# The expert stage of a two-block model on one core: a fixed TensorE order, biases in batches, and a last unit that joins as products

## The chip, the cores and the metric

The kernel runs on one core of a Trainium2 chip. A core has five engines with queues of their own: TensorE (PE), VectorE (DVE), ScalarE (ACT), GpSimd (POOL) and SyncE (SP, which here only issues transfers), and sixteen DMA engines. An engine takes the instructions of its queue in order. The metric is the device time of one launch in microseconds (us); less is better.

## What is computed

Two transformer blocks over T = 512 tokens of width D = 1024, all in float32. The first block has a mixer (a gated delta rule and sliding-window attention) and then 32 experts, of which each token takes four; the second has attention, an MLP, a recurrent layer and an MLP. The change lies in the experts:

```python
def _moe(h, w_router, b_router, w_up, b_up, w_down, b_down):
    logits = xf @ w_router + b_router              # 512 tokens, 32 experts
    top_val, top_idx = lax.top_k(logits, 4)
    gates = softmax(top_val)
    ...
    def expert_block(xb, e):                       # rows of one expert
        hu = xb @ w_up[e] + b_up[e]                # 1024 -> 2048
        x_glu = minimum(hu[:, :1024], 7.0)
        x_lin = clip(hu[:, 1024:], -7.0, 7.0)
        act = x_glu * sigmoid(1.702 * x_glu) * (x_lin + 1.0)
        return act @ w_down[e] + b_down[e]         # 1024 -> 1024
    ys = ys * row_gate[:, None]
    return segment_sum(ys, row_tok, num_segments=T)

x = x + gate2 * _moe(h, ...)
```

The weights of the experts are 384 MB (up 8 MB, down 4 MB for each expert), and all of them are read.

## The kernel before

**Ranks and units.** The experts are ranked by their count of tokens. A table, UNITS (L36), lays the ranks out in blocks of 128 rows: a block holds one expert (`_single`) or two (`_pair(a, b, n)`: n rows for a, the rest for b). One or two blocks that are worked on together are a step, one or two steps a unit; there are ten units with 20 blocks. Two of the units are a single step of two blocks (ranks 2 and 14, ranks 3 and 6). A rank's row count that the table doesn't hold goes to a loop over further blocks behind the second unit (LOOP, L1465), which runs zero times for these inputs. The last unit has the steps 23/24 and 13/31.

**One step.** `gather_T` (L1132) makes the transposed rows of a unit, xT, with products of the token matrix and 0/1 columns ("hot"). `expert_up` (L1159) makes for each quarter j of the 2048 columns a product in a PSUM bank "hu": first a product that puts in the biases (L1166), then the products with the weights (`tiled`, L1129), in tiles of 32, 64 or 128 columns by how the block is divided. DVE and ACT then apply the activation (L1176 to L1180: five operations, one on ACT), in place and into "ma". `transposed` (L1183) turns ma in eight transposes (L1188) and two copies (L1189) into aT, `expert_down` (L1192) makes the down product in two PSUM banks (hu for the second block of a step), and `expert_out` (L1203) scales the rows by their gates (ACT, L1208) and has POOL scatter them to y_d in DRAM (L1211). y_d has four slots for each token, 2048 rows in all. `slots` (L1113) makes row numbers and gates for the next unit. The down product of a step stands behind the up product of the step after it, in the code.

**What sets the order.** The code is written engine by engine in this sequence, but a scheduler orders each engine's queue, by dependencies and its own estimate, so PE's instructions of neighbouring steps are mixed. The weight loads (1 MB each, 384 of them) go to SP's queue in the order of the code, into thirteen buffers "raw" (L305). The hu banks are four, shared by all j and by the second block's down product.

**Ends of the stage.** Ahead of the stage SP fills half of y_d with zeros (L867, rows of slots that may stay empty). At its start the routing makes Z (positions and gates), transposes it (L1319), permutes it by rank (L1323) and derives R, selE and the like. `expert_bias` (L1397), called behind the first step of the last unit, adds the down biases to xs, the rows of the residual stream in h2h. At the end (L1472 on): SP loads the four slots of all tokens from y_d (`load_y`, L1474: 16 loads of 512 KB, four into h2l and twelve into raw buffers), DVE sums them (L1479), PE makes the last down product, that of 13/31, whose rows join as products with the hot columns instead of by a scatter (`add_rows`, L1215; products L1500 and L1501), and DVE adds these, multiplies by g2bc (gate2) and adds to xs (L1502 to L1504). The next stage starts with transposes of xs (L1580) and its weight loads on SP (L305).

## Time and profile before

| | us |
|---|---|
| median of the three runs | 2954.44 (2952.50 to 2954.49) |
| the profiled execution | 2947.46 |
| its span | 2945.2 |
| expert stage, first gather to first transposes of the next stage | 466.1 to 1613.4 |
| up to the end of the down product of 23/24 | 1549.4 |
| no PE work | 1549.4 to 1579.4 |
| last down product | 1579.4 to 1600.4 |
| sums to the next stage | 1600.4 to 1613.4 |

The profile shows one execution. Times in the timeline are counted from the start of its span. A timeline row gives the start, the length, the engine, the line, the operation with what it writes and reads, how many were run together, and in brackets the idle time before it and what ended that. A float32 product of the tiles here shows as two records in the trace: a quarter j of an up product of a block in tiles of 32 is 32 instructions and x64 in the timeline. A group's length runs to the modelled end of its last product; the next can start a little earlier, so distances between starts are the better measure.

### The profile page before, as it was taken

What the parts mean: (1) busy time and instruction counts of PE and PEld (TensorE: products, weight loads), DVE (VectorE), ACT (ScalarE), POOL (GpSimd) and SP (SyncE); (2) the same over time, 40 slices, a digit from 0 to 9 for tenths busy, and PEclk for the clock granted to TensorE, in tenths of its full rate; (3) what the DMA queues carried; (4) which work ended last, traced back from release to release, by engine and by line L of the source; (5) the groups of instructions that cost most, each with busy time, mean ns of one, the idle gap of its engine ahead of it and who ended that gap; (6) DMA issues with size and microseconds to landing.
All of it is one profiled execution on the core that took longest, in us unless ns stands there. A gap on an engine that the chain in (4) does not pass through costs nothing. (4 is left out here: it accounts for less than half of the span.)

```text
span 2945.2 us, 36638 instructions
## 1 busy us (share of the span) xinstructions
PE 2696.4 (92%) x14288; PEld 1713.3 (58%) x14288; DVE 1459.0 (50%) x2445; ACT 787.0 (27%) x1333; POOL 576.7 (20%) x401
## 2 busy tenths in 40 slices
PE   6889998998999999999994988999999899699997
PEld 4667875443434333333331756877877677588886
DVE  5996475211211111111124567676568788954446
ACT  4343341000000000000001553323235555332221
POOL 2340041000000000000000314233232333622223
PEclk8989998999999999999997998999998999799999
DMA  7544037797999997999986631565323222132331
GB/s 283 184 167 153 29 132 300 276 421 294 370 396 419 390 392 304 406 374 405 417 338 250 202 115 65 200 222 179 109 83 102 72 83 82 64 122 84 100 104 50
DMA packets 126209, 643.46 MB, mean 218 GB/s; under 512 B 16217, under 2 KB 17197, under 8 KB 76880
## 3 DMA queue, kind: packets, MB, share of 16 engines
q1 hardware_dynamic: 122064, 632.32, 57.0%
q0 software_dynamic: 3824, 8.25, 0.7%
q8 instruction: 113, 1.85, 0.3%
q14 instruction: 64, 0.52, 0.1%
q10 hardware_dynamic: 144, 0.52, 0.0%
HBM read 624.47 MB, written 18.45 MB: 218 GB/s over the span
## 5 line engine op out<-in xcount | busy, mean ns | idle before, releaser
L1129 PE MATMUL bank_hu<-raw,xT 128*32 128x512 f32 (+2 forms) x3456 | 618.2, 601 | 0.0
L1129 PEld LDWEIGHTS bank_hu<-raw,xT 128*32 128x32 f32 (+2 forms) x3456 | 190.0, 123 | 345.5 <-issue 336.4
L1603 POOL TENSOR_TENSOR h2h<-h2h,yt 128x512 f32<-128x512 f32 x161 | 239.5, 1494 | 679.7 <-DVE yt L1602 669.8
L319 DVE TENSOR_TENSOR wl<-raw,wh 128x1024 fp32r<-128x1024 f32 (+1 forms) x209 | 299.9, 1444 | 111.5 <-ACT wh L314 110.7
L314 ACT CAST wh<-raw 128x1024 fp32r<-128x1024 f32 (+1 forms) x231 | 236.8, 1042 | 399.1 <-PE bank_u L324 178.3
L1129 PE MATMUL bank_y<-raw,aT 128*32 128x512 f32 (+2 forms) x1536 | 294.7, 599 | 31.6 <-DMA raw<-in_w_down_dram 31.6
L1176 DVE TENSOR_SCALAR ma<-bank_hu 128x256 f32<-128x256 f32 x80 | 34.0, 425 | 561.3 <-PE bank_hu L1129 561.3
L324 PE MATMUL bank_u<-h_lo,wh 128*128 128x512 f32 (+1 forms) x680 | 250.8, 370 | 9.0 <-DVE h_lo L1587 9.0
L323 PE MATMUL bank_u<-h_hi,wh 128*128 128x512 f32 (+1 forms) x680 | 251.6, 372 | 7.1 <-ACT wh L314 4.1
L325 PE MATMUL bank_u<-h_hi,wl 128*128 128x512 f32 (+1 forms) x680 | 251.2, 370 | 3.6 <-DVE wl L319 3.6
L1211 POOL DMA_INDIRECT y_d<-yb,ii x19 | 18.6, 977 | 998.9 <-ACT yb L1208 865.8
L1129 PEld LDWEIGHTS bank_y<-raw,aT 128*32 128x32 f32 (+2 forms) x1536 | 95.5, 123 | 199.2 <-issue 189.4
L323 PE MATMUL bank_d<-wh,a 128*128 128x512 f32 x512 | 203.0, 397 | 3.5 <-DVE yt L1602 3.5
L1602 DVE TENSOR_TENSOR yt<-bank_d,G 128x512 f32<-128x512 f32 x168 | 113.4, 687 | 183.9 <-PE bank_d L325 178.3
L324 PE MATMUL bank_d<-wl,a 128*128 128x512 f32 x512 | 201.7, 394 | 0.7 <-DVE wl L319 0.7
L325 PE MATMUL bank_d<-wh,b 128*128 128x512 f32 x512 | 198.4, 394 | 1.0 <-DVE b L1822 1.0
L1177 ACT ACTIVATE mb<-ma 128x256 f32<-128x256 f32 x80 | 33.3, 417 | 582.2 <-DVE ma L1176 582.2
L324 PEld LDWEIGHTS bank_u<-h_lo,wh 128*128 128x128 f32 x680 | 130.4, 192 | 31.8 <-DVE h_lo L1587 9.8
L323 PEld LDWEIGHTS bank_u<-h_hi,wh 128*128 128x128 f32 x680 | 130.4, 193 | 29.2 <-ACT wh L314 4.5
L325 PEld LDWEIGHTS bank_u<-h_hi,wl 128*128 128x128 f32 x680 | 130.4, 192 | 26.1 <-DVE wl L319 3.8
L323 PEld LDWEIGHTS bank_d<-wh,a 128*128 128x128 f32 x512 | 96.7, 189 | 28.3 <-DVE yt L1602 5.2
L393 DVE SCALAR_TENSOR_TENSOR gacc<-graw,sc,gacc 128x1024 f32<-128x1024 f32 x67 | 91.4, 1364 | 42.5 <-DMA graw<-in_ada_w_dram 33.6
(568 smaller groups left out, 4403.3 us busy)
## 6 DMA issues: line engine op xcount, KB each, us to landing
raw<-in_w_up_dram SPq DMA_DIRECT2D x256, 1024.0 KB, 10.3
raw<-in_w_down_dram SPq DMA_DIRECT2D x128, 1024.0 KB, 12.6
raw<-in_mlp_w_dram SPq DMA_DIRECT2D x128, 512.0 KB, 4.4
graw<-in_ada_w_dram SPq DMA_DIRECT2D x72, 512.0 KB, 3.7
graw<-in_w_ada_dram SPq DMA_DIRECT2D x48, 512.0 KB, 4.5
raw<-in_ada_w_dram SPq DMA_DIRECT2D x24, 512.0 KB, 3.8
raw<-in_rnn_w_in_dram SPq DMA_DIRECT2D x24, 512.0 KB, 3.7
raw<-in_w_in_dram SPq DMA_DIRECT2D x22, 512.0 KB, 4.5
```

What stands on the lines that cost most here:

```text
L314: act.copy(out=h, in_=r)
L319: vec.tensor_tensor(out=l, in0=r, in1=h.bitcast(F), op=OP.subtract)
L323: pe.matmul(out=o, lhsT=lhs[0], rhs=rhs[0], start=first, stop=False)
L324: pe.matmul(out=o, lhsT=lhs[0], rhs=rhs[1], start=False, stop=False)
L325: pe.matmul(out=o, lhsT=lhs[1], rhs=rhs[0], start=False, stop=last)
L393: vec.scalar_tensor_tensor(out=acc, in0=r, scalar=w, in1=acc, op0=OP.mult, op1=OP.add)
L1129: pe.matmul(out=o[at + a:at + a + tile], lhsT=lhs[:, a:a + tile], rhs=rhs, start=start, stop=stop, tile_position=(0, at + a))
L1176: vec.tensor_scalar(out=a, in0=hu[:, 0:256], scalar1=7.0, scalar2=None, op0=OP.min)
L1177: act.activation(out=b, in_=a, func=AF.Tanh, scale=0.851)
L1211: pool.indirect_dma_start(out=y_d, out_offset=bass.IndirectOffsetOnAxis(ap=sl[0][:, 0:1], axis=0), in_=yb, in_offset=None, bounds_check=4 ...
L1602: vec.tensor_tensor(out=t, in0=ps, in1=G[:, cs], op=OP.mult)
L1603: eng.tensor_tensor(out=xs[tb][:, cs], in0=xs[tb][:, cs], in1=t, op=OP.add)
```

## The change

Eight things change, all in the expert stage.

1. The table of units is in a new order; the two units of two blocks now stand fifth and ninth (third and seventh before). The label permutation (which kept ranks 13 and 31 last) is gone, and ranks are used directly.
2. `pin` ties each PE instruction of the stage to the one pinned before it, in the order of the code. Pinned are biases, gathers, slots, weight products, transposes and the new late products; the routing transposes and expert_bias aren't.
3. The biases of a step are batched: all four j of a one-block step at its start, in the order 0, 2, 1, 3; for a two-block step j = 0 and 1 at the start, and j = 2 and 3 ahead of its third quarter.
4. The slots of the next unit are made between j = 1 and j = 2 of the last step.
5. The zero fill covers all of y_d, 16 loads rather than 8.
6. `add_slots`, called behind the first step of the last unit, loads the sixteen slot rows on POOL's queue into three pairs of buffers (two pairs in h2l, one in xT), and for each pair adds the two, multiplies by g2bc, and adds to xs: 24 DVE operations of 1024 columns.
7. Both blocks of the last unit, 23/24 and 13/31, join xs as products (`late_rows`, `late_add`), by halves of the width: DVE scales and multiplies by g2bc, ACT casts, DVE subtracts for the low part, PE makes two products into an hu bank for each of four token blocks, DVE adds to xs.
8. `load_y`, `sum_y` and the old tail are gone.

```diff
 UNITS = [
     [_single(0), _single(1)],
     [_pair(7, 25, 96), _pair(8, 26, 96)],
+    [_pair(15, 16, 64), _single(4)],
+    [_pair(9, 27, 96), _pair(17, 18, 64)],
     [[[(2, 0, 128, 0)], [(2, 0, 64, 128), (14, 64, 64, 0)]]],
-    [_pair(15, 16, 64), _pair(9, 27, 96)],
...
     [_pair(23, 24, 64), _pair(13, 31, 96)],
 ]
-LABELS = [r for r in range(32) if r not in (13, 31)] + [13, 31]
...
-    for tb in range(8, 16):
+    for tb in range(16):
         sync.dma_start(out=y_d[tb * 128:tb * 128 + 128, :]...
...
+    def pin(x):
+        if pinned[0] is not None:
+            tc.add_manual_dep(x.ins, pinned[0].name, mybir.DependencyInfo(
+                mybir.DependencyClass.NoSync, mybir.DependencyReason.DATA), reason="order")
+        pinned[0] = x.ins
...
+    def expert_up(srcs, biases, blocks, get=fetch, between=None):
         acts_ = [mt([128, 1024], "ma", 3, F, mo) for _ in blocks]
+        banks = {}
         for j in range(4):
-            hus = [pbank("hu") for _ in blocks]
-            q = slice(j // 2 * 64, j // 2 * 64 + 64)
-            for hu, bs in zip(hus, biases):
-                pe.matmul(out=hu, lhsT=bs[q], rhs=bup[q, j % 2 * 512:j % 2 * 512 + 512], start=True, stop=False)
+            if j not in banks:
+                js = (0, 2, 1, 3) if len(blocks) == 1 else (j, j + 1)
+                banks.update((j_, [pbank("hu") for _ in blocks]) for j_ in sorted(js))
+                for j_ in js:
+                    q = slice(j_ // 2 * 64, j_ // 2 * 64 + 64)
+                    for hu, bs in zip(banks[j_], biases):
+                        pin(pe.matmul(out=hu, lhsT=bs[q], rhs=bup[q, j_ % 2 * 512:j_ % 2 * 512 + 512], start=True,
+                                      stop=False))
+            if j == 2 and between is not None:
+                between()
+            hus = banks[j]
...
+    def late_rows(b):
+        hotT = mt([128, 1024], "ma", 3, FR, mo)[:, 0:512]
         pt = trbank()
         for tb in range(NTB):
+            pin(pe.matmul(out=pt[:, tbs[tb]], lhsT=hots[-1][:, tb, 128 * b:128 * b + 128].bitcast(F), rhs=ident,
+                          start=True, stop=True))
         act.copy(out=hotT, in_=pt)
+        return hotT
+
+    def late_add(y, gc, hotT):
+        yh, yl = (mt([128, 8, 128], "aT", 3, FR, mo).rearrange("p a b -> p (a b)") for _ in range(2))
         t_ = mt([128, 1024], "yb", 2, F, mo)
         for h in range(2):
             hs = slice(h * 512, h * 512 + 512)
+            vec.scalar_tensor_tensor(out=t_[:, hs], in0=y[h], scalar=gc, in1=g2bc[:, hs], op0=OP.mult, op1=OP.mult)
+            act.copy(out=yh[:, hs], in_=t_[:, hs])
+            vec.tensor_tensor(out=yl[:, hs], in0=t_[:, hs], in1=yh.bitcast(F)[:, hs], op=OP.subtract)
+            for tb in range(NTB):
+                o = pbank("hu")
+                pin(pe.matmul(out=o, lhsT=hotT[:, tbs[tb]], rhs=yh[:, hs], start=True, stop=False))
+                pin(pe.matmul(out=o, lhsT=hotT[:, tbs[tb]], rhs=yl[:, hs], start=False, stop=True))
+                vec.tensor_tensor(out=xs[tb][:, hs], in0=o, in1=xs[tb][:, hs], op=OP.add)
...
+    def add_slots():
+        spare = mt([128, 8, 256], "xT", 2).rearrange("p a b -> p (a b)")
+        pairs_ = [[h2_("l", 0), h2_("l", 1)], [h2_("l", 2), h2_("l", 3)], [spare[:, 0:1024], spare[:, 1024:2048]]]
+        for tb in range(NTB):
+            for j in (0, 2):
+                y = pairs_[0]
+                pairs_.append(pairs_.pop(0))
+                for i, t in enumerate(y):
+                    pool.dma_start(out=t, in_=y_d[(j + i) * T + tb * 128:(j + i) * T + tb * 128 + 128, :])
+                vec.tensor_tensor(out=y[0], in0=y[0], in1=y[1], op=OP.add)
+                vec.tensor_tensor(out=y[0], in0=y[0], in1=g2bc, op=OP.mult)
+                vec.tensor_tensor(out=xs[tb], in0=xs[tb], in1=y[0], op=OP.add)
...
+            late = not nxt and n
+            if late:
+                hotT = late_rows(n - 1)
             if prev is not None:
                 for y, sl in zip(expert_down(*prev[:2]), prev[2]):
                     finish()
-                    finish = expert_out(y, sl)
+                    if late:
+                        late_add(y, sl[1], hotT)
+                    else:
+                        finish = expert_out(y, sl)
...
             if not nxt and n == 0:
                 expert_bias()
+                add_slots()
...
-    load_y(ys[0], 0)
...
+    hotT = late_rows(1)
+    late_add(expert_down(*prev[:2])[0], prev[2][0][1], hotT)
```

How the instructions stand on the engines, in three places. In the rows, a name's number is that of its buffer.

PE before, one step in the middle of the stage (transposes of the step ahead, biases, up products bank_hu, slots bank_tr from R, then the down product bank_y):

```order
L1188 MATMUL bank_tr<-ident,ma 128x128 x8
L1166 MATMUL bank_hu<-bup,bs 128x512
L1129 MATMUL bank_hu<-raw,xT 32x512 x15
L1129 MATMUL bank_tr<-R,hot 128x2 x4
L1129 MATMUL bank_hu<-raw,xT 32x512 x17
L1166 MATMUL bank_hu<-bup,bs 128x512
L1129 MATMUL bank_hu<-raw,xT 32x512 x32
L1166 MATMUL bank_hu<-bup,bs 128x512
L1129 MATMUL bank_hu<-raw,xT 32x512 x32
L1166 MATMUL bank_hu<-bup,bs 128x512
L1129 MATMUL bank_hu<-raw,xT 32x512 x32
L1129 MATMUL bank_y<-raw,aT 128x512 x16
```

PE after, two steps of the same unit and its slots:

```order
L1203 MATMUL bank_tr<-ident,ma 128x128 x8
L1177 MATMUL bank_hu<-bup,bs 128x512 x4
L1134 MATMUL bank_hu<-raw,xT 32x512 x128
L1134 MATMUL bank_y<-raw,aT 128x512 x16
L1203 MATMUL bank_tr<-ident,ma 128x128 x8
L1177 MATMUL bank_hu<-bup,bs 128x512 x4
L1134 MATMUL bank_hu<-raw,xT 32x512 x64
L1134 MATMUL bank_tr<-R,hot 64x2 x8
L1134 MATMUL bank_tr<-R,hot 128x2 x4
L1134 MATMUL bank_hu<-raw,xT 32x512 x64
```

The four biases moved to the front of the step, and the up product is cut only by the slots of the next unit, at its half.

SP before, behind the first eight of the last sixteen down loads:

```order
L305 DMA raw<-in_w_down_dram 128x2048
L1474 DMA h2l_9937<-y_d 128x1024
L1474 DMA h2l_9938<-y_d 128x1024
L1474 DMA h2l_9939<-y_d 128x1024
L1474 DMA h2l_9940<-y_d 128x1024
L1474 DMA raw<-y_d 128x1024 x12
L305 ISA
L305 DMA raw<-in_w_down_dram 128x2048
```

After, the sixteen loads from y_d are gone from SP (the down loads follow each other) and stand on POOL behind its last scatter.

DVE after, behind the activations of the last up product (13/31): L1246 and L1248 scale and split the rows of 23/24, L1457 to L1459 are the sums of the slots, L1253 the additions of the late products:

```order
L1248 TENSOR_TENSOR aT<-yb,aT 128x512
L1246 SCALAR_TENSOR_TENSOR yb<-bank_y,gc,g2bc 128x512
L1248 TENSOR_TENSOR aT<-yb,aT 128x512
L1457 TENSOR_TENSOR h2l_9661<-h2l_9661,h2l_9662 128x1024
L1458 TENSOR_TENSOR h2l_9661<-h2l_9661,g2bc 128x1024
L1459 TENSOR_TENSOR h2h_9603<-h2h_9603,h2l_9661 128x1024
L1457 TENSOR_TENSOR h2l_9663<-h2l_9663,h2l_9664 128x1024
L1458 TENSOR_TENSOR h2l_9663<-h2l_9663,g2bc 128x1024
L1457 TENSOR_TENSOR xT<-xT 128x1024
L1459 TENSOR_TENSOR h2h_9603<-h2h_9603,h2l_9663 128x1024
L1458 TENSOR_TENSOR xT<-xT,g2bc 128x1024
L1253 TENSOR_TENSOR h2h_9603<-bank_hu,h2h_9603 128x512
```

All 24 sums stand behind the scaling of 23/24, and the eight late additions of 23/24 stand among them, the last two behind the last sum. On PE the sixteen late products of 23/24 (L1251, L1252) stand behind its down product and ahead of the transposes and the down product of 13/31.

## Rows read from the trace of the kernel before

**Rows 1.** The page, its first line.

```profile
span 2945.2 us, 36638 instructions
```

**Rows 2.** Windows: stretch, length; PE, PEld, DVE, ACT, POOL; clock, DMA, GB/s.

```profile
1200.00:1533.10 333.10, 322.17 (x2010) 116.91 (x2009) 60.08 (x133) 26.39 (x50) 9.56 (x9) 0.99 0.99 403
...
1549.40:1579.40 30.00, 0.03 (x1) 0.02 (x1) 14.71 (x12) 0.69 (x1) 0.97 (x1) 0.54 0.86 339
1579.40:1600.40 21.00, 19.32 (x128) 5.60 (x128) 0.00 (x1) 0.80 (x2) 0.00 (x0) 0.93 0.79 329
1600.40:1613.40 13.00, 4.02 (x17) 2.94 (x17) 11.91 (x16) 1.72 (x3) 0.00 (x0) 0.86 0.00 0
```

**Rows 3.** Timeline of PE, third and fourth blocks: start, length, line, operation, count.

```profile
563.89 3.63 PE L1129 MATMUL bank_hu<-raw,xT 128*32 128x512 f32 x30
567.45 1.05 PE L1129 MATMUL bank_tr<-R,hot 128*128 128x2 f32 x8
568.43 4.48 PE L1129 MATMUL bank_hu<-raw,xT 128*32 128x512 f32 x34
572.85 0.50 PE L1166 MATMUL bank_hu<-bup,bs 64*128 64x512 f32 x1
573.27 7.07 PE L1129 MATMUL bank_hu<-raw,xT 128*32 128x512 f32 x64
580.28 0.50 PE L1166 MATMUL bank_hu<-bup,bs 64*128 64x512 f32 x1
...
595.14 14.00 PE L1129 MATMUL bank_y<-raw,aT 128*128 128x512 f32 x32
608.98 1.04 PE L1188 MATMUL bank_tr<-ident,ma 128*128 128x128 f32 x8
```

**Rows 4.** Waits from 466 to 1613: us in total, times, the longest.

```profile
PE bank_tr L1188 <- DVE ma L1180: 14.8, 11, 2.0
```

**Rows 5.** Timeline, an activation chain on DVE, and products of PE behind such a wait.

```profile
1502.13 0.42 DVE L1176 TENSOR_SCALAR ma<-bank_hu 128x256 f32<-128x256 f32 x1 [1.67 <-PE bank_hu L1129]
...
1503.56 0.43 DVE L1180 SCALAR_TENSOR_TENSOR ma<-bank_hu,ma 128x256 f32<-128x256 f32 x1
...
1513.77 5.32 PE L1129 MATMUL bank_hu<-raw,xT 128*32 128x512 f32 x26
```

**Rows 6.** Timeline of PE, start of the stage: biases and the routing's permutation.

```profile
471.58 0.74 PE L1166 MATMUL bank_hu<-bup,bs 64*128 64x512 f32 x4
...
486.86 1.03 PE L1323 MATMUL bank_tr<-perm,ZT 96*128 96x96 f32 x8
```

**Rows 7.** Timeline of SP, the zero fill and the next weight loads behind it.

```profile
274.37 9.20 SPq L867 DMA_DIRECT2D y_d<-scb  x8
...
357.77 21.88 SPq L305 DMA_DIRECT2D raw<-in_w_out_dram  x8
```

**Rows 8.** Timeline, all engines, from the last scatter to the last down product.

```profile
1550.43 0.97 POOL L1211 DMA_INDIRECT y_d<-yb,ii  x1 [55.63 <-ACT yb L1208]
...
1566.65 3.80 DVE L1479 TENSOR_TENSOR raw<-raw 128x1024 f32<-128x1024 f32 x3 [1.34 <-DMA raw<-y_d]
1567.97 9.27 SPq L305 DMA_DIRECT2D raw<-in_w_down_dram  x8
```

**Rows 9.** Timeline, from the last down product to the next stage.

```profile
1602.79 0.68 DVE L1502 TENSOR_TENSOR h2l<-bank_hu,h2l 128x512 f32<-128x512 f32 x1
...
1613.25 3.49 DVE L1504 TENSOR_TENSOR h2h<-h2h,raw 128x1024 f32<-128x1024 f32 x3
1613.39 1.97 PE L1580 MATMUL bank_t<-ident,h2h 128*128 128x128 f32 x8 [8.43 <-DVE h2h L1504]
```

**Rows 10.** DMA issues: tile, queue, kind, count, KB each, us to landing.

```profile
raw<-y_d SPq DMA_DIRECT2D x12, 512.0 KB, 9.9
h2l<-y_d SPq DMA_DIRECT2D x4, 512.0 KB, 3.7
y_d<-yb,ii POOLq DMA_INDIRECT x19, 8.8
```

More of the change, by code (lines that the diff above doesn't have):

```diff
@@ L38 @@
     [_pair(7, 25, 96), _pair(8, 26, 96)],
+    [_pair(15, 16, 64), _single(4)],
+    [_pair(9, 27, 96), _pair(17, 18, 64)],
     [[[(2, 0, 128, 0)], [(2, 0, 64, 128), (14, 64, 64, 0)]]],
[L40 to L41 removed]
     [_pair(10, 28, 96), _pair(19, 20, 64)],
+    [_pair(11, 29, 96), _single(5)],
+    [_pair(12, 30, 96), _pair(21, 22, 64)],
     [[[(3, 0, 128, 0)], [(6, 0, 96, 0), (3, 96, 32, 128)]]],
[L44 to L45 removed]
     [_pair(23, 24, 64), _pair(13, 31, 96)],
 ]
[L49 to L50 removed]
 CAPS = [0] * 32
@@ L54 @@
         for _blk in _step:
-            for _label, _, _n, _ in _blk:
-                CAPS[_label] += _n
+            for _rank, _, _n, _ in _blk:
+                CAPS[_rank] += _n
 SQRT2 = 2.0 ** 0.5
@@ L1139, in gather_T @@
                     for tb in range(NTB):
-                        pe.matmul(out=pt[:, j * n:j * n + n], lhsT=h2s[part][tb][:, (k + j) * 128:(k + j + 1) * 128],
-                                  rhs=hot[tb], start=part + tb == 0, stop=part == 1 and tb == NTB - 1)
+                        pin(pe.matmul(out=pt[:, j * n:j * n + n], rhs=hot[tb],
+                                      lhsT=h2s[part][tb][:, (k + j) * 128:(k + j + 1) * 128],
+                                      start=part + tb == 0, stop=part == 1 and tb == NTB - 1))
             (vec.tensor_copy if k % 4 else act.copy)(out=X[:, k:k + 2, :],
@@ L1224, in add_rows @@
             hs = slice(h * 512, h * 512 + 512)
-            t = t_[:, hs]
-            act.activation(out=t, in_=y[h], func=AF.Copy, scale=gc)
-            act.copy(out=yh[:, hs], in_=t)
-            vec.tensor_tensor(out=yl[:, hs], in0=t, in1=yh.bitcast(F)[:, hs], op=OP.subtract)
-        return hotT, yh, yl
+            vec.scalar_tensor_tensor(out=t_[:, hs], in0=y[h], scalar=gc, in1=g2bc[:, hs], op0=OP.mult, op1=OP.mult)
[6 more added lines that the diff above has]
+                vec.tensor_tensor(out=xs[tb][:, hs], in0=o, in1=xs[tb][:, hs], op=OP.add)
     def expert_w(ex):
@@ L1266, in step_of @@
     def step_of(step, X, b0):
-        labels = []
+        ranks = []
         for blk in step:
-            labels += [part[0] for part in blk if part[0] not in labels]
-        ws = [ranked(label) for label in labels]
-        places = [([part[1:3] for part in blk], [labels.index(part[0]) for part in blk]) for blk in step]
+            ranks += [part[0] for part in blk if part[0] not in ranks]
+        ws = [ranked(rank) for rank in ranks]
+        places = [([part[1:3] for part in blk], [ranks.index(part[0]) for part in blk]) for blk in step]
         tile_ = min(32 if part[2] == 96 else part[2] for blk in step for part in blk)
@@ L1429, in tile_block @@
             up, down, blocks = step_of(step, X, b0)
-            if n == 0 and nxt:
+            biases = [bias_of(blk) for blk in step]
+            parts = []
+            if n + 1 == len(unit) and nxt:
                 hot_unit()
-            biases = [bias_of(blk) for blk in step]
-            for b in range(n * len(nxt) // len(unit), (n + 1) * len(nxt) // len(unit)):
-                sls_.append(block_rows(b, nxt[b]))
-            au = expert_up(up, biases, blocks)
+                parts = [block_rows(b, blk) for b, blk in enumerate(nxt)]
+            au = expert_up(up, biases, blocks, between=lambda: sls_.extend([slots(p_) for p_ in parts]))
             if u == 0 and n == 0:
```

76 lines of the change are left out of this document (21 added, 55 removed).

## The prediction

> **What bounds the kernel now.** I began with the page for the span, 2945.2 us [rows 1]; the profiled execution took 2947.46 us, and the runs' median is 2954.44, so 7.0 us are added to what I work out for the profiled one. Then I cut the expert stage (466 to 1613 us) into stretches by the windows [rows 2]. From 1200.0 to 1533.1 PE is busy 322 of 333 us at a granted clock of 0.99, with DMA at 0.99 and 403 GB/s: PE bounds this stretch, with the weight stream close behind. From 1549.4 to 1579.4 PE does nothing, from 1579.4 to 1600.4 it does the last block's down product, and from 1600.4 to 1613.4 the block's rows are added and PE does hardly anything. So the time can come from what PE does up to 1549.4 (end of the down product of ranks 23/24), and from the 64 us behind that.
>
> How full is the busy part? In PE's timeline [rows 3] one j of an up product, undisturbed, takes 7.01 us (573.27 to 580.28), a block's down product 13.84 (595.14 to 608.98). Up to 1549.4 stand 20 blocks' up products and 19 down products: 20 x 4 x 7.01 + 19 x 13.84 = 824 us. Gathers, biases, transposes, slots and one 9 us wait at the overflow loop make some 160 more. The stretch lasts 1549.4 - 466.1 = 1083 us, so about 100 us are neither. They are the target. Three kinds can be seen. First, a group that is cut by a foreign one loses time at each cut: at 563.89, x30 and x34 with slots between last from 563.89 to 572.85, 8.96 us, of which the slots own 0.98; 7.98 against 7.01, 1.0 us for one cut [rows 3]. Cuts of other shapes cost less; over the stage I count about 46 us. Second, PE waits for the activation chain on DVE, ahead of pairs of transposes: eleven waits of 14.8 us in all [rows 4], and PE drains for about half a us ahead of each, some 20 us. Third, after such a wait PE is at the lower of its two clocks (1.2 GHz) for a while: x26 at 1513.77 takes 5.32 us [rows 5] where 26 of 64 at 7.01 would take 2.85, so 2.5 us each; about 10 us in the stage.
>
> **The change, part by part.** *Pinned order.* The order of the changed program shows whole groups (an up product as x128 behind four biases) and the eight transposes in a row behind a whole down product, so DVE's chain, four operations of 0.42 us and one on ACT, from 1502.13 to 1503.99 [rows 5], has 14 us of cover where it had none. I take back 46 (cuts), 20 (waits) and 6 of the 10 (clock), since some waits remain. If that cover were gone, the 2 us per wait would return.
>
> *Batched biases.* Alone, a bias takes 0.42 us (572.85 to 573.27) [rows 3]; four in a row take 0.74 in the first step [rows 6]. 80 of them: 34 us to 15. I take -19, and -4 for transposes eight in a row. Against it: (1) in the first unit the experts' matmuls now stand behind the routing transposes and slots, which were done between them (perm at 486.86 [rows 6]); the way through ACT and DVE has to be waited for: +3. (2) A two-block step takes all four hu banks for its first two j, so the second batch of biases waits for DVE and ACT on both blocks of j = 1: twice the chain of 1.86 us [rows 5], 3.7 us for each of two such steps: +7. (3) After a two-block down product the hu banks must be emptied by ACT: +4. (4) The stream: the bytes are the same, and PE now asks for them faster. At 403 GB/s [rows 2] a load of 1 MB takes 2.6 us. A block that two experts share needs 24 loads, 62 us, for some 48 us of PE; a block of one expert 12 loads, 31 us. Thirteen buffers even out a part of this; followed load by load in this arithmetic, with 2.5 to 2.6 us a load, PE waits 15 to 40 us in all. I take +16, since the stream lies ahead at the start (DMA 0.99 only from the second stretch on), and 5 to 40 as bounds.
>
> Sum: -95 + 30 = -65: the down product of 23/24 ends near 1484.
>
> *Zero fill.* It grows from 8 to 16 loads on SP, 9.2 us more [rows 7]; up to 357.77 SP has only a few small loads behind it, so it costs nothing. Without that hole, 9 us.
>
> *The hole at the end.* Before, the last scatter (1550.43) must land, then SP issues sixteen loads, and only then the eight weight loads for the last down product, at 1567.97; PE starts at 1579.4 [rows 2, 8]. In the changed order on SP the last sixteen down loads stand in a row, and the sixteen row loads go to POOL behind the scatters of the unit ahead, under the last up product. So the 30 us hole goes, and the 21 us product, which waits for its loads one by one, becomes 14.
>
> *What is late next.* This is where I expect much of it to go. In the changed order on DVE the sums of the rows (24 operations 1024 wide) stand behind the scaling of 23/24, that is behind its down product, and the late additions between them. The second half of the late products needs hu banks that these additions free, and PE is pinned: the last down product stands behind them. Hence, from the end of the down product: scaling, cast and subtraction for two halves, about 4 us (six operations of 512 columns, some 0.68 each [rows 9]); 24 sums at 1.2 us (three in 3.49 us [rows 9]; the same with 1.27 between starts at 1566.65 [rows 8]) 28.8; seven additions at 0.6, 4.2; then one product 0.9, eight transposes and copy 2.1, down product 14.0, lower clock after the wait 2.5 [rows 5]: 56.6 us, so the last down product ends at 1484 + 56.6 = 1540.6 where it was 1600.4.
>
> *Row loads.* They are 512 KB each in three pairs of buffers; before a pair is needed again two others are summed, 2 x 3.5 us and late additions, about 8.6 us. The trace has no load of this size issued by POOL. Nearest rows: the same loads from SP took 3.7 us first in line and 9.9 in a queue of twelve, POOL's scatters 8.8 [rows 10]. So each of five reloads is between free and late by 1.3, or later if the issue is slow: 0 to 20 us, and I take 2, near the first, because at that time only few other loads run. It can't gain, since the sums bound from the other side. The Trainium skill, page "DMA: Bandwidth & Descriptors", section on the anatomy of one DMA on the SWDGE path, gives 2.0 us plus bytes over 436 GB/s for such a load, an estimate of 3.2 us; by it nothing would be late and the sum would be 2 us smaller. No run here shows it yet.
>
> *Behind the last down product.* Before: 13.0 us to the first transposes of the next stage, at 1613.39, held by three adds per token block [rows 9]. After: scaling and cast 2, five products and one addition, 4.5: about 6.5. The next stage's weights can be issued 2 us earlier, too. So the first transposes come at about 1540.6 + 2 + 6.5 = 1549, minus 2 for the weights: 66 us earlier, and everything behind is unchanged.
>
> Sum against the profiled run: 2947.5 - 66 = 2881; with 7: **2888**.
>
> **Rivals.** *Sums off the path* (0.08): if the loads land early and DVE takes the sums under the last up product, the wait of 30 us goes: end near 1512 instead of 1541, 2858. Against it: the order on DVE is a queue, and the sums stand behind work that needs the down product. *Row loads late* (0.2): POOL builds these loads while DVE is dense; if each of the five reloads comes 2 to 4 us late, 2898 to 2908. For it speaks the 8.8 us of the scatters [rows 10], against it the 3.7 us of the first four loads there and that the weights' queue is nearly empty by then. The Trainium skill, page "SBUF — State Buffer", warns that a DVE copy from SBUF to SBUF can keep GpSimd from writing descriptors, but says that tensor_tensor does not; the sums are tensor_tensor, so by it this rival is the weaker. *The stream binds* (0.14): the +16 is +35 and more, or the pins stall PE where the free order filled in with other work (in the two-block steps above all): the stage gains only 30 to 45 us, 2908 to 2925. *Slower* (0.06): the row loads are served one after another and not six at a time. 16 loads at the scatters' 8.8 us are 141 us from about 1440, the last scatter of the unit ahead; then come the last sums (4 us), the last product and transposes (3), the down product at first at the lower clock (16.5) and the additions (6.5): first transposes at 1611, about as now (1613.4). From 9.4 us a load on it is slower by more than 0.2%: 2955 to 2975. *It doesn't do what it says* (0.03): the pins hold nothing and the old pattern returns; then only the hole goes, 2905 to 2955. Against it stands the changed order itself.
>
> **How the numbers follow.** The forecast (2872 to 2900) has 0.49, the rivals 0.51. 0.2% is 6 us, about what a measurement of this kernel can tell from no change. All cases but the slow rival and part of the last lie more than 6 us below 2954: faster 0.91, same 0.03, slower 0.06. The range reaches from the first rival's 2858 to the upper end of the third, 2925.
>
> **What would show it.** Right: unbroken x64 groups of 7.07 us and hardly any wait of transposes for DVE; down(23/24) ending at 1475 to 1495; then PE idle some 30 us in the late products, released by DVE's additions, while the 1024-wide sums run back to back; no wait for down weights at the last product; first transposes near 1548. Wrong: the sums running before the end of that down product (first rival), gaps on DVE released by row loads (second), waits for weights all through the stage (third).

## The result, and the profile after

The changed kernel takes 2891.51 us (median; 2891.10 to 2891.91) against 2954.47 us for the kernel before, taken beside it: a ratio of 0.9782, 95% interval 0.9766 to 0.9799. The forecast was 2888, 3.5 us lower. The profiled execution has a span of 2890.0 us against the 2945.2 us of [rows 1]; the same points in both traces:

| us from the start of the span | before | after | predicted |
|---|---|---|---|
| first gather of the stage | 466.1 | 467.1 | |
| first expert matmul | 474.2 | 484.4 | 477 |
| end of the down product of 23/24 | 1549.4 | 1489.2 | 1484 |
| last down product | 1579.4 to 1600.4 | 1536.0 to 1549.9 | to 1540.6 |
| first transposes of the next stage | 1613.4 | 1555.2 | 1549 |
| from the end of 23/24 to there | 64.0 | 66.0 | 65 |

The last row says where the gain is **not**: the new end of the stage, from rows summed ahead to late products, is no shorter than the old one. All of the 58 us come from ahead of the end of 23/24. (Behind the stage the two executions differ by 3 us, 1331.8 against 1334.8, where nothing was changed.)

The pins do to PE what its order said. The timeline of PE after, the block that [rows 3] showed cut up (start, length, line, operation, count):

```profile
568.37 0.73 PE L1177 MATMUL bank_hu<-bup,bs 64*128 64x512 f32 x4
569.03 27.67 PE L1134 MATMUL bank_hu<-raw,xT 128*32 128x512 f32 x256
596.63 14.00 PE L1134 MATMUL bank_y<-raw,aT 128*128 128x512 f32 x32
```

Four quarters in 27.67 us are 6.92 each, less than the 7.01 of an undisturbed one before. But PE's waits, from 466 to 1560 us (total, times, longest), are other ones:

```profile
PE bank_hu L1251 <- DVE h2h L1253: 35.2, 4, 14.6
PE bank_hu L1177 <- DVE bs L1287: 16.6, 1, 16.6
PE bank_hu L1134 <- DMA raw<-in_w_up_dram: 13.8, 14, 1.3
PE bank_y L1134 <- DMA raw<-in_w_down_dram: 9.2, 6, 2.7
...
PE bank_tr L1203 <- ACT aT L1204: 0.5, 2, 0.3
```

The 14.8 us of [rows 4] are gone: no transpose waits for DVE any more. In their place stand 23 us of waits for weights, of which the trace before has none in the same stretch. The windows after (stretch, length; PE, PEld, DVE, ACT, POOL busy; granted clock as a share of the full one; DMA share, that is the mean busy share of the sixteen DMA engines; GB/s) say the same; in [rows 2] the share was 0.99 at 403 GB/s:

```profile
466.00:562.00 96.00, 92.56 (x394) 53.69 (x395) 28.18 (x105) 6.84 (x14) 0.00 (x0) 0.94 0.72 270
...
676.00:1200.00 524.00, 503.08 (x3188) 211.70 (x3192) 94.21 (x247) 41.60 (x81) 10.65 (x11) 0.99 0.99 410
1200.00:1460.00 260.00, 254.54 (x1876) 99.23 (x1869) 54.55 (x126) 22.51 (x43) 10.95 (x13) 0.99 0.99 408
1460.00:1500.00 40.00, 26.61 (x128) 8.77 (x120) 12.07 (x16) 2.24 (x4) 1.59 (x3) 0.90 1.02 420
1500.00:1510.00 10.00, 1.19 (x2) 0.50 (x2) 6.61 (x7) 0.00 (x0) 2.11 (x4) 0.50 1.02 414
1510.00:1520.00 10.00, 1.22 (x2) 0.50 (x2) 6.89 (x8) 0.00 (x0) 1.20 (x3) 0.50 0.73 273
```

From 562 to 1510 us the DMA engines have little room left; the widest gap is at the overflow loop (0.84 from 660 to 690). The end of the stage on PE (in brackets the idle time ahead, and what ended it):

```profile
1466.14 4.50 PE L1134 MATMUL bank_y<-raw,aT 128*64 128x512 f32 x18
1472.77 4.84 PE L1134 MATMUL bank_y<-raw,aT 128*64 128x512 f32 x16 [2.12 <-DMA raw<-in_w_down_dram]
1480.32 8.86 PE L1134 MATMUL bank_y<-raw,aT 128*64 128x512 f32 x30 [2.70 <-DMA raw<-in_w_down_dram]
...
1502.73 0.77 PE L1251 MATMUL bank_hu<-aT,ma 128*128 128x512 f32 x1 [10.31 <-DVE h2h L1253]
...
1518.48 0.79 PE L1251 MATMUL bank_hu<-aT,ma 128*128 128x512 f32 x1 [14.55 <-DVE h2h L1253]
...
1535.97 13.94 PE L1134 MATMUL bank_y<-raw,aT 128*32 128x512 f32 x128
```

The down product of 23/24 takes 23 us instead of 14; 4.8 of the 9 us are waits for its weights in these rows, and some 2 more go with a stretch at the lower clock behind them (granted 0.50 from 1482 to 1484). Then PE waits for DVE's additions, as predicted, and the last down product waits for nothing, at 13.94 us against the 21 in [rows 2]. DVE in the same stretch:

```profile
1492.44 1.22 DVE L1457 TENSOR_TENSOR h2l<-h2l,h2l 128x1024 f32<-128x1024 f32 x1
...
1505.97 1.23 DVE L1457 TENSOR_TENSOR h2l<-h2l,h2l 128x1024 f32<-128x1024 f32 x1 [3.39 <-DMA h2l<-y_d]
...
1513.19 1.23 DVE L1457 TENSOR_TENSOR h2l<-h2l,h2l 128x1024 f32<-128x1024 f32 x1 [3.11 <-DMA h2l<-y_d]
...
1530.46 0.69 DVE L1253 TENSOR_TENSOR h2h<-bank_hu,h2h 128x512 f32<-128x512 f32 x1
```

The sums run from 1492.4 on, with two gaps, 6.5 us in all, in which a row load is late.

### The profile page after: what moved, and what is told of

It reads as the page before. It is cut to its first block, busy times and chain, and to the rows that moved or that the text cites. A ratio compares the mean times of both kernels' runs of the same rounds, so it can differ in the third digit from the quotient of the medians.

```text
span 2890.0 us, 36724 instructions
## 1 busy us (share of the span) xinstructions
PE 2621.3 (91%) x14312; PEld 1713.5 (59%) x14312; DVE 1473.1 (51%) x2463; ACT 785.8 (27%) x1332; POOL 580.3 (20%) x416
## 4 chain that ended last, share of the span: by engine, by line
PE 48%; DMA 13%; DVE 11%; ACT 2%; issue 2%; POOL 0%; DVEq 0%; SPq 0%; ACTq 0%
PE bank_hu L1134 11%; DMA raw<-in_w_up_dram 6%; PE bank_y L1134 5%; PE bank_d L319 5%; PE bank_d L321 5%; PE bank_d L320 5%; DMA raw<-in_w_down_dram 4%; PE bank_u L321 4%; PE bank_u L320 4%; PE bank_u L319 4%; DVE wl L315 2%; PE bank_tr L1145 2%; DMA graw<-in_ada_w_dram 1%; DVE vv L1951 1%; DVE h_lo L1603 1%
## 5 line engine op out<-in xcount | busy, mean ns | idle before, releaser
L1134 PE MATMUL bank_hu<-raw,xT 128*32 128x512 f32 (+2 forms) x3456 | 571.9, 597 | 13.8 <-DMA raw<-in_w_up_dram 13.8
L1134 PEld LDWEIGHTS bank_hu<-raw,xT 128*32 128x32 f32 (+2 forms) x3456 | 201.8, 124 | 364.6 <-issue 324.4
L1134 PE MATMUL bank_y<-raw,aT 128*32 128x512 f32 (+2 forms) x1536 | 259.9, 596 | 9.3 <-DMA raw<-in_w_down_dram 9.2
L1134 PEld LDWEIGHTS bank_y<-raw,aT 128*32 128x32 f32 (+2 forms) x1536 | 84.5, 124 | 173.8 <-issue 154.8
L1204 DVE COPY aT<-bank_tr 128x512 f32<-128x512 f32 x20 | 13.8, 692 | 245.1 <-PE bank_tr L1203 245.1
## 6 DMA issues: line engine op xcount, KB each, us to landing
raw<-in_w_up_dram SPq DMA_DIRECT2D x256, 1024.0 KB, 19.4
```

The costliest lines, as they stand in the source:

```text
L1134: pin(pe.matmul(out=o[at + a:at + a + tile], lhsT=lhs[:, a:a + tile], rhs=rhs, start=start, stop=stop, tile_position=(0, at + a)))
```

## Experiments: what made the stage shorter

*The theory with which I began (A)* is the prediction's: PE's time bounds the stage, so each edit that takes time from PE gives that time. *The rival (B)*: PE's cuts were what kept it behind the weight stream; once they are gone, the stream sets the stage, and further savings on PE turn into waits for weights. Times are medians; ratios, with a 95% interval, are to the kernel before, run beside each (2952 to 2957 us), so small differences are read from the ratios.

**The pins taken out.** All other edits stay.

```diff
     def pin(x):
-        if pinned[0] is not None:
+        if False:
```

> The changed kernel without the pins: the scheduler orders PE again, all else the same (biases in batches, new units, sums and last unit). Theory A (the gain comes from unbroken groups and covered activation chains, so from the pins): cuts and waits return, the down product of 23/24 ends 30 to 50 us later, 2920 to 2945. Rival B (the weight stream sets the stage at the rate PE frees its buffers; cuts hide behind it): 5 to 15 us slower, 2896 to 2907. Rival C (the gain comes from the tail and the order of units, the pins give nothing): 2888 to 2895.

2952.19 us (ratio 1.0001, 0.9992 to 1.0011): nothing is left of the gain. The stage waits again as in [rows 4], and 23/24 ends at 1553.9:

```profile
PE bank_tr L1203 <- DVE ma L1195: 17.5, 13, 2.0
PE bank_hu L1177 <- DVE bs L1287: 12.8, 1, 12.8
```

I had expected to keep 10 to 35 us, for the hole at the end. The last down product does end earlier, at 1573.9 instead of 1600.4, but PE then waits for the sums behind it, and the next stage starts at 1622.8, 68.8 us behind the end of 23/24 (64.0 before). So with a free order the new end of the stage brings nothing of its own.

**The pins alone**, in the kernel before: `pin` around its biases, gathers, products and transposes.

```diff
-            pe.matmul(out=o[at + a:at + a + tile], lhsT=lhs[:, a:a + tile], rhs=rhs, ...)
+            pin(pe.matmul(out=o[at + a:at + a + tile], lhsT=lhs[:, a:a + tile], rhs=rhs, ...))
...
```

> The kernel before with the pins alone, on the same kinds of instruction, in the order of its code; units, biases, row loads on SP and the tail as before. From the end of the down product of 23/24 to the next stage the old tail takes 64 us and the new one 66, so if the pins alone bring the stage's gain of 60 us, it takes 2893 to 2905. If batches and the order of units carry half of it, 2915 to 2930. If pins in the old code make PE wait (a bias at each j for its bank), 2930 or more.

2913.94 us (0.9864, 0.9845 to 0.9883): 40 of the 63 us. The prediction had 72 for what pinning removes; the trace shows what came instead, PE's waits from 466 to 1560 us:

```profile
PE bank_y L1138 <- DMA raw<-in_w_down_dram: 44.6, 16, 28.0
PE bank_tr L1138 <- SPq L1475: 13.7, 1, 13.7
PE bank_hu L1138 <- DMA raw<-in_w_up_dram: 6.5, 5, 1.3
```

28.0 of the 44.6 are the hole at the end and 4 more lie in the last down product; the rest of the two rows, 19 us, are waits for weights in the stage, where the kernel before has none.

**The old order of units** in the kernel after.

```diff
     [_pair(7, 25, 96), _pair(8, 26, 96)],
-    [_pair(15, 16, 64), _single(4)],
-    [_pair(9, 27, 96), _pair(17, 18, 64)],
     [[[(2, 0, 128, 0)], [(2, 0, 64, 128), (14, 64, 64, 0)]]],
+    [_pair(15, 16, 64), _pair(9, 27, 96)],
+    [_pair(17, 18, 64), _single(4)],
...
```

> The changed kernel with the order of units of before (two-block steps third and seventh, as the sequence was). The prediction gave the order of units no term of its own: 2888 to 2897. If the order matters because a two-block step asks for fewer bytes per PE time, and so lets the stream catch up where it is behind, 5 to 15 us slower, 2897 to 2907.

2910.51 us (0.9848, 0.9831 to 0.9864): 19 us slower than after, more than either case of the expectation gave it. The prediction had no term for the order. Windows of the old order and, below it, of the kernel after:

```profile
676.00:800.00 124.00, 114.19 (x648) 44.44 (x650) 23.06 (x65) 8.19 (x17) 1.94 (x2) 0.93 0.79 312
```

```profile
676.00:800.00 124.00, 118.97 (x716) 48.20 (x720) 22.90 (x62) 9.04 (x18) 2.92 (x3) 0.96 0.97 403
```

In the old order the two-block unit of ranks 2 and 14, with 24 loads for two blocks, stands right behind the overflow loop. The stream stands idle there a fifth of the time (0.79; the kernel before had 0.81, and so has the pinned one): PE works on and frees few of the thirteen buffers. The units that follow need 24 loads for each block of two experts and have PE wait: 27.6 us for up weights instead of 13.8. In the new order, units that need many loads come first, and the light one fifth, when the stream is behind and the light unit lets it catch up. Share lost is 0.18 x 124 = 22 us, and 19 is what the time shows. Both two-block units move in this edit; which of the two places counts for how much, no run shows.

**Biases quarter by quarter**, in the kernel after.

```diff
-                js = (0, 2, 1, 3) if len(blocks) == 1 else (j, j + 1)
+                js = (j,)
```

> The changed kernel with the biases taken one j at a time, ahead of each j, as before the change, all else the same. Theory A (PE's own work sets the stage): 80 biases at 0.42 us in place of 0.18, so 15 to 20 us slower, 2906 to 2912. Rival B (the stream of weights sets the stage, DMA share 0.99 to 1.02 from 600 us on): at most 5 us slower, 2890 to 2897; the two-block steps may even gain, since the second batch no longer waits.

2893.77 us (0.9784, 0.9767 to 0.9802): within what can be told from no change. The prediction gave the batches 19 us. Without them the waits for up weights are 4.0 us instead of 13.8 and the wait at the loop 12.3 instead of 16.6: what PE saves, it waits.

**38 us of PE work taken out.** The gather's products with the low halves of the tokens are left out.

```diff
-                for part in range(2):
+                for part in range(1):
...
```

> The changed kernel without the low halves in the gather (320 of its 640 products are left out, so the gathered rows are less exact): 320 x 0.118 = 38 us less work on PE, no byte less of weights. Theory A: 30 to 38 us faster, 2853 to 2862. Rival B: the weights come no faster, only stalls of the stream that PE causes go: 5 to 15 us faster, 2876 to 2887, and PE's waits for weights grow by 20 us or more.

2881.92 us (0.9746, 0.9728 to 0.9764): 9.6 of 38 us (in the traces, from the first gather to the end of 23/24, it is 12.9). This tells A from B: a quarter to a third of what PE saves comes out as time. Most of the rest is in its waits:

```profile
PE bank_hu L1134 <- DMA raw<-in_w_up_dram: 21.1, 20, 1.4
PE bank_hu L1177 <- DVE bs L1287: 20.1, 1, 20.1
PE bank_y L1134 <- DMA raw<-in_w_down_dram: 13.7, 9, 2.7
```

They make 55 us, against 40 in the kernel after. With 3 us of a later first gather in this trace that accounts for about 19 of the 28 us that are missing; for the others I name no row.

**No overflow loop.** The loop, which runs zero times, is left out; with it goes the wait at its door. In the kernel after, PE is idle there until 681.03, behind DVE, and DVE behind SP:

```profile
680.68 0.64 DVE L1287 CAST bs<-selE 128x64 fp32r<-128x64 f32 x5 [15.54 <-SPq L1511]
681.03 1.22 PE L1177 MATMUL bank_hu<-bup,bs 64*128 64x512 f32 x4 [16.62 <-DVE bs L1287]
```

The last weight load ahead of the loop is issued at 660.0, and an up load takes 19.4 us to land (10.3 us before); together that is 679.4, just ahead of DVE's row. In the kernel before the wait was shorter:

```profile
PE bank_tr L1129 <- SPq L1465: 8.7, 1, 8.7
```

So it looks like a wait for all loads on the way, which grew because the queue is fuller; no run isolates this.

```diff
-    LOOP = 1
+    LOOP = -1
```

> The changed kernel without the loop over further blocks behind the second unit, which runs zero times for these inputs. PE waits 16.6 us there (8.7 before), until SP's loads issued ahead have landed. Theory A (PE's work sets the stage): those 16.6 us go, 2873 to 2878. Rival B (the stream sets the stage; it loses about 5 us there): 2883 to 2889.

2883.70 us (0.9767, 0.9748 to 0.9786): 8 us by the medians, 4 by the ratios, whose intervals overlap, so no gain is told apart. The traces show none in the stage either: from the first gather to the end of 23/24 it takes 1022 us in both. The stream is full where the loop stood (421 GB/s from 660 to 690, against 339), but the waits for weights grow from 23.0 to 34.0 us.

**An earlier start.** In the kernel after, the first unit's slots stand between the routing and the first expert matmul. Moved inside the first step:

```diff
-    sls = [slots([(0, hot0[b], lambda tb: R[:, tb, b, :])]) for b in range(2)]
+    sls = []
...
+            ... between=first_slots if u + n == 0 else lambda: ...
```

> The changed kernel with the slots of the first unit made inside the first step, at its half, rather than ahead of it: the first products with weights start near 476 rather than 484.4, so the weight buffers come free 8 us earlier while the stream stands (DMA share 0.72 from 466 to 562). If the stream sets the stage, these 8 us of idle stream are gained: 2882 to 2886. If the stage is set by PE's work and waits later on, also some 8 us; but if it is lost again (a later idle stretch of the stream grows, at the loop or in the two-block steps): 2888 to 2893.

2887.96 us (0.9783, 0.9767 to 0.9800). The first expert matmul starts 8.5 us earlier and 23/24 ends 3.4 us earlier, of which 1.5 were there at the first gather; the medians differ by 3.5 us and the ratios by nothing. So the expectation's last case holds: what the stream gains at the start it loses again. One place is the first two-block step (below, this kernel and then the kernel after), where PE has much work for few bytes and the stream stands idle:

```profile
900.00:950.00 50.00, 48.70 (x286) 30.31 (x284) 12.64 (x37) 3.68 (x8) 0.00 (x0) 0.97 0.83 339
```

```profile
900.00:950.00 50.00, 48.70 (x294) 29.99 (x292) 11.81 (x36) 3.68 (x8) 0.00 (x0) 1.00 0.94 386
```

So (B) holds for most of the stage but not for all of it: in this step PE, busy 48.70 of 50 us, comes last.

## Experiments: what sets the end of the stage

After 23/24, PE waits 35.2 us for additions that stand among 24 sums. The first theory (A) was that the order on DVE alone holds them back; the rival (B), that the rows come late. Two kernels order DVE anew.

**All 24 sums ahead of the scaling of 23/24, and only the first three pairs ahead:**

```diff
-            vec.scalar_tensor_tensor(out=t_[:, hs], in0=y[h], scalar=gc, ...)
+            x = vec.scalar_tensor_tensor(out=t_[:, hs], in0=y[h], scalar=gc, ...)
+            if sums:
+                tc.add_manual_dep(x.ins, sums[-1].name, ...)
...
+                if len(sums) < 8:          # 3 in the second kernel
+                    sums.append(x.ins)
```

> The changed kernel (2891.5 us) with one order added on DVE: all 24 sums of the slot rows stand ahead of the scaling of 23/24, so they can run while PE is still in the down product of 23/24. Theory A (the sums lie on the path, as predicted: PE is idle 35.2 us in the late products, released by DVE's additions): the first three pairs are summed before that product ends, PE's idle time in the late products shrinks to 10 to 20 us and the kernel takes 2866 to 2880. Rival B (the weight stream sets the end: the last down loads land near 1500, and the row loads share the stream, so the sums come no earlier): 2886 to 2895, with DVE waiting for row loads among the sums.

> As e1_all_ahead, but only the sums of the first three pairs (those that need no reload) stand ahead of the scaling of 23/24; the rest stays behind it as in the changed kernel. Theory A: nine sums at 1.2 us leave the path and the reloads are issued some 15 us earlier: 10 to 20 us less, 2871 to 2882, at least as good as all ahead, since the late additions need not wait for the reloads. Rival B: 2886 to 2895.

2887.40 us (0.9762, 0.9745 to 0.9779) and 2889.49 us (0.9768, 0.9746 to 0.9791): not told apart from the kernel after. The sums now wait for their rows instead: 29.1 and 25.5 us, against 6.5. And the rows, asked for earlier, come between the weights of 23/24, which ends 5 us later (1494.3 and 1494.7).

**All rows asked for early.** The reloads wait for buffers of the sums; with five "raw" buffers for the last five pairs, on top of the order with all 24 sums ahead, they need not.

```diff
+                        add_slots(3, [(r[:, 0:1024], r[:, 1024:2048]) for r in
+                                      [m_raw.tile([128, 2048], F, tag="raw", name="raw") for _ in range(5)]])
```

> As e1_all_ahead, but only the first three pairs of slot rows use the old buffers; the other five are loaded into weight buffers that are free once the last up product is done, so no row load waits for a sum. In e1_all_ahead DVE waited some 34 us for row loads among the sums. Theory A (the turn of three buffer pairs, a load issued only when a sum is done, sets the sums' end): all rows land near 1500, the sums end near 1503 in place of 1525.7, and the kernel takes 2866 to 2876. Rival B (rows and weights share one stream that is full until 1520 anyway, and the last down loads now come later): 2882 to 2890.

2885.44 us (0.9777, 0.9761 to 0.9793), not told apart from the kernel after. Its windows, two of its sums on DVE, and its DMA issues (tile, queue, count, size, median us to landing):

```profile
1500.00:1510.00 10.00, 0.00 (x0) 0.00 (x0) 5.56 (x5) 0.00 (x0) 0.00 (x0) 0.50 1.02 419
1510.00:1520.00 10.00, 0.00 (x0) 0.00 (x0) 3.50 (x3) 0.00 (x0) 0.00 (x0) 0.50 0.89 365
...
1499.43 1.23 DVE L1460 TENSOR_TENSOR raw<-raw 128x1024 f32<-128x1024 f32 x1 [3.80 <-DMA raw<-y_d]
...
1506.99 1.22 DVE L1460 TENSOR_TENSOR raw<-raw 128x1024 f32<-128x1024 f32 x1 [3.82 <-DMA raw<-y_d]
...
raw<-y_d POOLq DMA_DIRECT2D x10, 512.0 KB, 29.7
```

The stream is full until about 1519 with DVE half idle: the rows (8 MB in all) share it with the last weights, a pair every 7.5 us, and the last come with the last weights. A sum can't run before its rows are there, whatever the order on DVE.

**The rows ahead of the last eight weights**: the same ten loads on SP's queue, between the down loads of 23/24 and those of 13/31.

```diff
-                pool.dma_start(out=t, in_=y_d[(j + i) * T + ...
+                queue.dma_start(out=t, in_=y_d[(j + i) * T + ...      # sync for the last five pairs
```

> The kernel after, with the slot sums put ahead of the scaling of steps 23 and 24, as in e10_raw_rows, and with the ten rows of the last five pairs loaded on SP's queue, between the down weights of steps 23 and 24 and those of steps 13 and 31, rather than on POOL's. Theory A (the rows of the old slots stand at the very end of one stream with the last weights: in e10_raw_rows a pair came every 7.5 us, and the last about 1519, and the first transposes of the next stage at 1554.0): with their place in the stream set ahead of the last eight weights, the rows come first, the weights follow at 2.49 us each while DVE adds, and the tail falls to the stream's own length: the stream of before the next stage is the same bytes, so its end stays near 1521, the last down product then ends about 14 us of PE work later at most, 1528 to 1535, and the first transposes of the next stage about 1530 to 1537: 2862 to 2871 us. Theory B (the order in the stream makes no difference, because the scatter of the old slots, or DVE's own chain of sums, sets when the late products can be added): 2882 to 2890 us. Worse than B (over 2892): SP stands still behind the first row load until the last scatter has landed, and the eight weights behind it come late by that.

2882.32 us (0.9746, 0.9726 to 0.9766), at the lower edge of the second theory's band, and by one of the reasons that it names, DVE's chain. The rows do come earlier (DVE is busy 10.00 of the 10 us from 1500 on, where it was 5.56), but the first theory had forgotten the 27 us that 24 sums take on DVE:

```profile
1491.40 1.23 DVE L1460 TENSOR_TENSOR raw<-raw 128x1024 f32<-128x1024 f32 x1 [22.61 <-DMA raw<-y_d]
...
1496.21 1.22 DVE L1460 TENSOR_TENSOR h2l<-h2l,h2l 128x1024 f32<-128x1024 f32 x1
...
1513.36 1.23 DVE L1462 TENSOR_TENSOR h2h<-h2h,raw 128x1024 f32<-128x1024 f32 x1
1514.50 1.40 DVE L1246 SCALAR_TENSOR_TENSOR yb<-bank_y,gc,g2bc 128x512 f32<-128x512 f32 x2
...
1515.95 0.80 PE L1256 MATMUL bank_hu<-aT,ma 128*128 128x512 f32 x1 [23.68 <-ACT aT L1252]
1530.60 13.94 PE L1134 MATMUL bank_y<-raw,aT 128*32 128x512 f32 x128
```

Twenty sums back to back, then the scaling, then the late products. The last down product starts at 1530.6, against 1534.8 with the same rows on POOL.

The 22.61 us ahead of the first sum are a matter of the order on DVE after all. Its queue has a pair of "raw" first, and the first pairs, in h2l, behind it, though these had been there since about 1477 at the latest (issued by POOL from 1455.9 to 1459.6, landed in at most 17.1 us); in the kernel with all rows on POOL's queue the first of them was summed at 1469.3:

```profile
1469.28 1.23 DVE L1460 TENSOR_TENSOR h2l<-h2l,h2l 128x1024 f32<-128x1024 f32 x1 [0.50 <-DMA h2l<-y_d]
```

What sums of these pairs ahead of the "raw" ones would gain, no run shows.

**Together**: the same, with the gains multiplied in at the scaling of the scattered rows, so that 16 sums are left of 24, and with the early start.

```diff
-            act.activation(out=yb[:, n * 512:n * 512 + 512], in_=y[n], func=AF.Copy, scale=sl[1])
+            vec.scalar_tensor_tensor(out=yb[:, n * 512:n * 512 + 512], in0=y[n], scalar=sl[1],
+                                     in1=g2bc[:, n * 512:n * 512 + 512], op0=OP.mult, op1=OP.mult)
...
-            vec.tensor_tensor(out=y[0], in0=y[0], in1=g2bc, op=OP.mult)
```

> e12_sp_rows, with two more edits: the expert outputs of the scattered slots are multiplied by the per-column gains in their scaling on VectorE, so that the eight multiplications among the 24 slot operations go (8 x 1.2 = 9.6 us of DVE behind the rows, for 36 more scalings that move from ScalarE to DVE beside other work), and the first unit's slot lists are made inside its first step, as in e11_early_start (which alone gave 3.5 us). Theory A (the rows' place in the stream was what held the tail): 2852 to 2865 us. Theory B (it was not, see e12_sp_rows): 2879 to 2888 us. If the two extra edits add nothing to e12_sp_rows, the two agree within 4 us.

2872.02 us (2869.71 to 2876.51; ratio 0.9718, 0.9697 to 0.9739): the fastest kernel here, some 19 us below the kernel after. It lies between the two bands, so neither theory had its size. In its trace 23/24 ends at 1484.9 (7.4 us earlier than with the rows on SP alone, of which 2.4 were there at the first gather), and the late products start here:

```profile
1500.81 1.40 DVE L1247 SCALAR_TENSOR_TENSOR yb<-bank_y,gc,g2bc 128x512 f32<-128x512 f32 x2
...
1502.26 0.79 PE L1257 MATMUL bank_hu<-aT,ma 128*128 128x512 f32 x1 [17.37 <-ACT aT L1253]
...
1517.56 13.94 PE L1134 MATMUL bank_y<-raw,aT 128*32 128x512 f32 x128
```

The late products come 13.7 us earlier, 7.4 by the earlier end and some 6 by the shorter chain, of the 9.6 that eight operations take. From the end of 23/24 to the next stage it is 51.8 us, against 66.0 after and 64.0 before. Here too DVE stands idle 21.3 us ahead of the first sum, which is of a "raw" pair.

## Why the prediction was right, and where its terms were not

The time and the way to it came out close: 23/24 ended 5 us later than predicted, the next stage began 6 us later, and the end of the stage was as long as before because the sums took the place of the hole. But the sum for the stage was right by terms that were wrong in both directions; that they cancelled was luck. So was a part of the step from the stage to the time: the profiled execution of the kernel before lay 7.0 us below its median and these were added, while the profiled execution after (2891.91) lies at its median. From one profiled execution to the other the gain is 55.6 us, where 66 was forecast.

- *Pins: -46 for cuts, -20 for waits, -6 for the clock.* The mechanism is shown (x256 in 27.67 us; no waits of transposes for DVE; without pins no gain). How much of it belongs to cuts, waits and clock, no run tells apart. The size was that of PE's own time. Alone the pins gave 40 us.
- *Biases and transposes, -19 and -4.* Mis-sized as a gain: undoing the batches costs 2 us, not distinguishable from none. PE did save the time and spent it in waits for weights.
- *The order of the units, no term.* It was worth 19 us, by keeping the stream at 0.97 behind the loop. The prediction listed the bytes of each kind of unit, and put the waits that follow from them at a flat +16; it did not follow the buffers unit by unit under both orders.
- *The stream, +16 with bounds 5 and 40.* Waits for weights are 23.0 us, inside the bounds. But this was the step that should have come first: since PE asks faster than the stream delivers, it is not a cost beside the others, it limits them all together: leaving out 38 us of PE work gave 9.6. The third rival described this, and without the new order of units it would have been the outcome: 2910.5 us, in its range of 2908 to 2925.
- *The start, +3.* The first expert matmul comes 10.2 us later than before; moving the slots back gave 8.5 us of it at the start, and no gain in time that is told apart.
- *Second batch of biases in two-block steps, +7; hu banks, +4.* PE waits 0.98 and 0.32 us for DVE in the second batch of such a step, 2.6 us in both steps. The hu banks show no wait of their own.
- *The loop, unchanged.* Its wait grew from the 8.7 us of the kernel before to 16.6, which the prediction had no term for; without the loop the stage was no shorter in the trace.
- *The late chain, 56.6 us.* From the end of 23/24 to that of the last down product: 60.7 us. By steps: scaling to the first sum 4.1 (predicted 4), of which 0.8 lie ahead of the modelled end of 23/24; sums and additions 32.2 without the gaps (33.0); gaps for rows 6.5 (2); late product and transposes 4.8, at the lower clock (3.0); the down product 13.94, at the upper clock (16.5). The sums back to back on the path, the core of the prediction, are right.
- *Row loads.* I took 2 us from bounds of 0 and 20 because "only few other loads run" at that time. That reason failed: the stream is at 1.02 until 1510, and the loads took 9.4 us in the median (16.2 for those into xT), near the bound of 9.9 in [rows 10] and not the 3.7 that I leaned to. The issues of the kernel after:

```profile
h2l<-y_d POOLq DMA_DIRECT2D x12, 512.0 KB, 9.4
...
xT<-y_d POOLq DMA_DIRECT2D x4, 512.0 KB, 16.2
```

The Trainium skill's fit (page "DMA: Bandwidth & Descriptors", section on the anatomy of one DMA on the SWDGE path), from which 3.2 us was estimated, is not what the trace shows here: 9.4 us, beside weights that keep the DMA engines full.

- *Behind the last down product, 6.5 us:* 5.2. The 2 us for earlier weight loads of the next stage don't show: what lies behind is 3 us longer. *Zero fill, nothing:* the first gather starts 1.0 us later, no more than executions of the same work differ (464.4 to 470.5 in the traces here).

## What to carry to other kernels

Ask first which stream a faster engine would catch up with, and treat it as a limit on the sum of all savings, not as one more cost; an experiment that leaves out a slice of the engine's work measures directly how much of a saving is left (9.6 of 38 us here). Where work with many bytes and work with few alternate over a ring of buffers, put the light steps where the stream is behind: their place alone was worth 19 us here. And when a hole at the end is filled by moving work ahead, follow the loads of the moved work too: here they shared the stream with the last weights, and the last came with them.

## What the runs showed of the hardware

- Rows read back beside a full weight stream got a third of it: 3.94 MB in 28 us are 141 GB/s, and the weights meanwhile got 276 GB/s, where, almost by themselves, they had 421 (1200 to 1300 us in the kernel after). The DMA queues (packets, MB, share of 16 engines) from 1490 to 1518 us, in the kernel with five raw buffers on POOL's queue:

```profile
q1 hardware_dynamic: 1058, 7.72, 66.2%
q0 software_dynamic: 1080, 3.94, 35.3%
```

q1 carries the weights, q0 the rows. Both move about as many packets; a packet of the weights is twice as long in the mean (7.3 and 3.6 KB). The Trainium skill (page "DMA: Bandwidth & Descriptors", section "SWDGE vs HWDGE vs iDMA") says that a DMA engine goes round its queues in turn, and the trace agrees: 1058 packets against 1080 (767 against 766 from 1470 to 1490). Here the second queue got its share by packets, not by who asked first.

- The same load on the same queue took 9.4 us where its issue waits for a buffer (median of twelve), and 29.7 us where ten are asked for in a row, with nothing won in time: the landing time was a place in a line.
- Cutting a group of products by a foreign one cost PE 1.0 us in [rows 3], and whole groups ran 0.09 us for each quarter faster than the "undisturbed" ones of before.
- After a wait of some 24 us PE's late products ran at 0.63 us (0.39 at the end of the stage) at a granted clock of 0.50, the lower of the two levels (1.2 GHz), in the kernel with the rows on SP; behind another 4.6 us of waiting, six products and sixteen transposes its down product of 13.94 us ran at a granted clock of 1.00 (2.4 GHz).
